# Two gate tiles of a state space decoder: half of their products computed inside the state space stage

## Chip, cores and metric

The kernel runs on one core of a Trainium2 chip. The metric is device time in microseconds (us) of one execution, the median of several runs. Lower is better. One execution was also recorded by the hardware profiler; all rows below are from it. TensorE is called PE, VectorE DVE, ScalarE ACT, GpSimd POOL, and SyncE, which issues most transfers, SP.

## The reference

A two-layer decoder trunk on one sequence of 1024 tokens with 1024 features: a diagonal state space layer with a gate, an MLP, a stick-breaking attention layer, a second MLP, with layer norms between. The change is in the first layer's mixer, cut here to what matters:

```python
def s5_mixer(x, w_in, ..., w_glu, b_glu, w_out):
    u = (x @ w_in).reshape(bsz, seq, S5_GROUPS, S5_GROUP)     # 64 groups of 16 channels
    ...
    _, _, s_re, s_im = lax.associative_scan(combine, (a_re, a_im, bu_re, bu_im), axis=0)
    y = (jnp.einsum('lbgp,ghp->blgh', s_re, c_re) - jnp.einsum('lbgp,ghp->blgh', s_im, c_im))
    y = (y + d_skip * u).reshape(bsz, seq, D_MODEL)
    g = jax.nn.gelu(y)
    out = g * jax.nn.sigmoid(g @ w_glu + b_glu)
    return out @ w_out
```

`g @ w_glu` is a product of 1024 x 1024 by 1024 x 1024; its sum over the 1024 input features runs over 8 tiles of 128 features.

## The kernel before

All large products are done in a three-product form: each operand is split into a high and a low part (`split`: a cast on ACT, a subtraction on DVE), and high times high, high times low and low times high are added in PSUM. A weight arrives by a transfer on SP's queue into a raw buffer (three of them, pool `wr`), is split into a slot of a weight pool (`wa` or `wb`, four slots each, a slot for 128 x 512 with both parts), and the raw buffer is free again.

**The state space stage** runs in 16 steps, one for each `Half` n of four groups (the loop from -3 to 16 overlaps three steps). The program text of a step has these parts: `into` and `scan` of half n+1 (PE: `p` from `U` and `V`; DVE: `R`, a scan, and then `Rs` and `Rc`), `y_mm` of half n (PE: `py`, 12 products from `Dm`, `Rc` and `Rs`), `kern` of half n+1 (PE: `pk`; ACT: four copies to `Dm`), transposes of half n+2 (`pU`, `pv`, copied by ACT to `U`, `V` and `Vs`), then the gelu of half n (ACT square `gs`, DVE, ACT tanh, DVE `zt`). After every second half, `z_out(i)` transposes a finished tile i of 128 features on PE (`pz`), and ACT and DVE write its high and low part, `gT_h` and `gT_l`. The gate reads `gT`.

Between those parts `fill` issues other work for PE. In steps before `NE` = 6 it is the rest of the input projection (`bunits`). In steps 6 to 14 it is nothing. In the last two steps it is the beginning of the gate (`gunits`, from `glu_ahead`): for the output tiles f = 0 and 1 the products of the feature tiles k = 0 to 6, six matmuls of 128x512 for one k (three products, two halves of the tokens), in numbers given by `GS`:

```python
def glu_ahead():
    for f in range(2):
        glu_ps(f)
        for k in range(KD - 1):
            dense_fm(pg[f], wg[f], gT, [k])
            yield
GS = (6, 1, 1, 1, 0), (3, 2, 0, 0, 0)
```

The weights of f = 0 and 1 are in `wa` from step 6 on.

**The gate** follows: k = 7 of f = 0 and 1, then f = 2 to 7 with all eight k. `glu_out(f)` does a sigmoid on ACT from PSUM (`gt`), a product with g on DVE (POOL has added up g in `zg`), and a split into `gg`. Weights are loaded two tiles ahead; those of f = 2 and 3 go into `wb`. After it come the output projection (`sopy`) and the MLP (`m0...`, where `wa` and `wb` take turns as slots for the weights).

The order of instructions on each engine is set by a scheduler from the program order and from when it takes buffers and inputs to be ready, so that an added part can also change the order of its neighbours. PSUM has eight banks: in this stage two for each of the tags `p12`, `pv`, `py` and `u`; `pz` uses `u`.

Of the kernel before, what the change touches and what calls it, by code (L numbers as in the profile page):

```python
# [9 lines left out]
F32 = mybir.dt.float32  # L10
# [35 lines left out]
def trunk(ctx, tc, A, out):  # L46
# [51 lines left out]
    def half(h):  # L98
        return slice(h * HF, (h + 1) * HF)
# [1 line left out]
    def tok(t):  # L101
        return slice(t * P, (t + 1) * P)

    def dense_fm(ps, w, xa, ks=range(KD), hs=(0, 1)):
        for k in ks:
            wh, wl = w[k]
            for h in hs:
                pe.matmul(ps[h], wh, xa[0][:, k, half(h)], start=(k == 0), stop=False)  # L108
            for h in hs:
                pe.matmul(ps[h], wh, xa[1][:, k, half(h)], start=False, stop=False)  # L110
            for h in hs:
                pe.matmul(ps[h], wl, xa[0][:, k, half(h)], start=False, stop=(k == KD - 1))
# [27 lines left out]
    class Slots:  # L140
# [8 lines left out]
        def next(self):  # L149
            self.n += 1  # L150
            return self.pools[(self.n - 1) % len(self.pools)]

        def of(self, src, name):

            return load_w(self.next(), None, name, HF, src)[0]

    def rows2(w, j, cols):

# [124 lines left out]
    with ExitStack() as ph:  # L283
# [380 lines left out]
                u_out(1, j, ps)  # L664


        wg, pg = {}, {}

        def glu_w(f):
            wg[f] = by_k(wsl.load(A["w_glu"][f], f"glu{f}"))  # L670
# [1 line left out]
        def glu_ps(f):  # L672
            pl, tag = ((ps1, "p12"), (ps1, "pv"), (ps1, "py"), (psu, "u"))[f % 4]
            pg[f] = [pl.tile([P, HF], F32, tag=tag, name=f"pg{f}{h}") for h in range(2)]

        def glu_ahead():
            for f in range(2):
                glu_ps(f)
                for k in range(KD - 1):
                    dense_fm(pg[f], wg[f], gT, [k])  # L680
                    yield

        tabs, zts = {}, {}
        NH = 2 * KD
        NE = 6
        GS = (6, 1, 1, 1, 0), (3, 2, 0, 0, 0)
        FS = (2,1,1,1,1)
        H = [Half(n) for n in range(NH)]
        for _ in stage_b([0]):
# [3 lines left out]
        for n in range(-3, NH + 1):  # L693
            cur = H[n] if 0 <= n < NH else None
            nx = H[n + 1] if 0 <= n + 1 < NH else None
            nx2 = H[n + 2] if 0 <= n + 2 < NH else None
            nx3 = H[n + 3] if n + 3 < NH else None

            def fill(i):
                if n < NE:  # L700
                    for _ in range(FS[i]):
                        next(bunits, None)
                elif n >= NH - 1:
                    for _ in range(GS[n - NH + 1][i]):
                        next(gunits, None)

            if n == NE:
                for _ in bunits:
                    pass
                rs_.close()  # L710
                gT = act_tiles(actp, "act", "gT")
                raws.append(mkpool(ctx, "wr", 3, side="right"))
                wa = mkpool(ctx, "wa", 4, side="right")
                wsl = Slots([wa] * 2)
                for f in range(2):
                    glu_w(f)
                gunits = glu_ahead()
            if nx3:
                load_bc(n + 3)
            if nx:  # L720
                nx.decay()
                nx.into()
                nx.scan()
            fill(0)
            if cur:
                cur.y_mm()
            fill(1)
            if nx:
                nx.kern()
            fill(2)  # L730
            if nx2:
                nx2.u_trans()
                nx2.v_coef()
            fill(3)
            if nx2:
                nx2.v_trans()
                nx2.w_coef()
            if cur:
                cur.gelu1()
            fill(4)  # L740
            if nx3 and nx3.hh == 0:
                tabs[nx3.i] = outer_tables(nx3.i)
            if n >= NE:
                if zwait:
                    z_out(zwait.pop(0))
            if cur:
                cur.gelu2()
            if cur and cur.hh == 1:
                zwait.append(cur.i)

    wb = mkpool(wbs, "wb", 4, side="right")
    wsl.pools += [wb] * 2


# [267 lines left out]
    class Down:  # L1022
# [21 lines left out]
        def tile(self, pl, nm_, tag):  # L1044
            return pl.tile([P, HF], F32, tag=tag, name=f"{self.nm}{nm_}")
# [274 lines left out]
    with ExitStack() as ph:  # L1320
        with ExitStack() as ph1:
            bp = mkpool(ph1, "ggp", 4)
            gg = act_tiles(bp, "gg", "gg")
            yst = ExitStack()
            yp = mkpool(yst, "yp", 8)
            y_tiles = [yp.tile([P, D], F32, tag="y", name=f"y0_{t}") for t in range(8)]
            with ExitStack() as ph2:
                zp = mkpool(ph2, "gz", 2)

                def glu_out(f, ps):  # L1330
                    for h in range(2):
                        z = zp.tile([P, HF], F32, tag="z", name=f"zg{f}{h}")
                        pool.tensor_add(z, gT[0][:, f, half(h)], gT[1][:, f, half(h)])
                        gt = zp.tile([P, HF], F32, tag="gt", name=f"gt{f}{h}")
                        act.activation(gt, ps[h], AF.Sigmoid, bias=bglu[:, f:f + 1])
                        dve.tensor_mul(gt, gt, z)

                        src = gt.rearrange("p (j c) -> p j c", j=4)
                        hv, lv = [v[:, f].rearrange("p (c j) -> p j c", j=8)[:, 4 * h:4 * h + 4] for v in gg]
                        split(hv, lv, src)  # L1340

                wo = []

                def ahead(i):
                    if i < KD:
                        glu_w(i)
                    else:
                        wo.append(wsl.load(rows2(A["w_out"], i - KD, half(0)), f"so0{i - KD}"))

                for f in range(KD):  # L1350
                    ahead(f + 2)
                    if f < 2:
                        dense_fm(pg[f], wg[f], gT, [KD - 1])
                    else:
                        glu_ps(f)
                        dense_fm(pg[f], wg[f], gT)
                    if f == KD - 1:
                        ahead(KD + 2)
                    glu_out(f, pg[f])
                ahead(KD + 3)  # L1360
            glu.close()

            def y_load(t):
                dma.dma_start(y_tiles[t], A["x"][tok(t)])

            xo = XOps(actp, "x1")
            w1 = []
            with ExitStack() as ph2:
                rest = proj_ln(ph2, flat(wo), lambda j: wsl.load(rows2(A["w_out"], j, half(1)), f"so1{j}"),
                               gg, xo, x_d[0], y_load, A["lnmg"][0], A["lnmb"][0], "so", y_tiles, w1_ahead(0, w1))  # L1370
            vpr = VProject()
            down = Down(0, "d0", x_d[0], wb, False, vpr)
            mlp_up(0, xo, y_tiles, w1, "m0", yst, bp, "gg", wb, "right", rest, down)
        with ExitStack() as ph1:
            x2T = down.run(ph1)
# [280 lines left out]
```

## Time and profile before

| | |
|---|---|
| runs, median of 3 | 2390.17 us (2385.36 to 2396.45) |
| profiled execution | 2393.1 us, span from first to last instruction 2391.4 us |
| PE busy | 2276.9 us, 95% of the span |
| DVE busy | 1838.9 us, 77% |
| ACT busy | 1234.1 us, 52% |
| POOL busy | 415.7 us, 17% |
| mean granted TensorE clock | 0.983 |

The shares are means over the whole span. The state space stage, the gate and the MLPs have different limits, so the stages have to be read apart. A busy time of PE sums records that overlap, because matmuls are pipelined; the pace of matmuls is read from their starts.

### The profile page before, as it was taken

The numbers are of one execution on the slowest core, as the hardware profiler recorded it, in microseconds if no ns is written. First come the engines' busy times: TensorE is split into PE (matmuls) and PEld (weight loads), VectorE is DVE, ScalarE is ACT, GpSimd is POOL, SyncE is SP. The second block draws the span as 40 slices with busy tenths as digits, with TensorE's granted clock in tenths as the row PEclk, the third lists the DMA queues.
The fourth block names the chain that finished last, engine by engine and source line by source line (L and its number), as shares of the span: only waits on it lengthen the run. The fifth ranks groups of instructions, "written<-read, shape, count | busy, mean of one in ns | idle before, by whom it ended". The sixth has DMA issues, their size and how long they took to land.

```text
span 2391.4 us, 32754 instructions
## 1 busy us (share of the span) xinstructions
PE 2276.9 (95%) x11072; PEld 1864.7 (78%) x11072; DVE 1838.9 (77%) x2887; ACT 1234.1 (52%) x2365; POOL 415.7 (17%) x709
## 2 busy tenths in 40 slices
PE   8997999999999999999999999988989999999996
PEld 7776878777888788888878878766867888788885
DVE  8899564886665888788179999896887666687888
ACT  6566441475555444444156777673366555544443
POOL 4000220021111000001144444341002111100002
PEclk9998999999999999999999999999999999999998
DMA  4222231385444944536655554465457434665432
GB/s 148 65 78 54 68 105 66 137 276 182 145 148 161 316 129 146 150 97 185 128 130 120 127 124 112 117 144 190 141 182 277 154 146 145 231 201 167 134 114 106
DMA packets 195448, 349.38 MB, mean 146 GB/s; under 512 B 23248, under 2 KB 66256, under 8 KB 195280
## 3 DMA queue, kind: packets, MB, share of 16 engines
q1 hardware_dynamic: 136400, 246.61, 33.0%
q0 software_dynamic: 58880, 100.69, 15.2%
q8 instruction: 87, 1.43, 0.3%
q14 instruction: 81, 0.66, 0.1%
HBM read 212.96 MB, written 100.66 MB: 131 GB/s over the span
## 4 chain that ended last, share of the span: by engine, by line
PE 59%; DVE 14%; issue 12%; DMA 5%; ACT 4%; POOL 4%; SPq 0%; POOLq 0%; DVEq 0%; ACTq 0%
PE d0M L1109 4%; PE d0M L1111 4%; PE d0M L1110 4%; PE d1M L1109 4%; PE d1M L1111 4%; PE d1M L1110 4%; DVE qq L1470 2%; PE m0A L847 2%; PE m0A L846 2%; PE m0A L845 2%; DVE be L1471 2%; POOL h_d L939 2%; PE po L1497 1%; PE pg L108 1%; PE pg L110 1%
## 5 line engine op out<-in xcount | busy, mean ns | idle before, releaser
L1470 DVE TENSOR_TENSOR_SCAN qq<-qq 128x128 f32<-128x128 f32 (+7 forms) x128 | 173.8, 1360 | 11.4 <-POOL qq L1464 11.2
L1109 PE MATMUL d1M<-w_d12M,w_d1HM 128*128 128x512 f32 x448 | 175.0, 392 | 2.6 <-DVE d1y L1118 2.6
L1109 PE MATMUL d0M<-w_d02M,w_d0HM 128*128 128x512 f32 x448 | 174.6, 390 | 1.4 <-ACT w_d02M L122 1.0
L1111 PE MATMUL d1M<-w_d12M,w_d1HM 128*128 128x512 f32 x448 | 175.2, 391 | 0.0
L1110 PE MATMUL d1M<-w_d12M,w_d1HM 128*128 128x512 f32 x448 | 174.7, 390 | 0.0
L1110 PE MATMUL d0M<-w_d02M,w_d0HM 128*128 128x512 f32 x448 | 174.5, 390 | 0.0
L1111 PE MATMUL d0M<-w_d02M,w_d0HM 128*128 128x512 f32 x448 | 174.3, 389 | 0.0
L122 ACT CAST w_d0HM<-d0hM 128x512 fp32r<-128x512 f32 x110 | 68.3, 621 | 169.0 <-PE d0M L1111 140.0
L122 ACT CAST w_d1HM<-d1hM 128x512 fp32r<-128x512 f32 x110 | 68.3, 621 | 168.2 <-PE d1M L1111 136.1
L122 ACT CAST wTh<-pt 128x512 fp32r<-128x512 f32 (+1 forms) x192 | 88.0, 485 | 82.7 <-PE pt L1483 82.1
L1483 PE MATMUL pt<-ident,be 128*128 128x128 f32 x576 | 91.0, 282 | 35.4 <-DVE wTl L123 26.5
L1483 PEld LDWEIGHTS pt<-ident,be 128*128 128x128 f32 x576 | 70.0, 144 | 61.8 <-issue 15.5
L123 DVE TENSOR_TENSOR w_d1HM<-d1hM,w_d1HM 128x512 fp32r<-128x512 f32 x110 | 75.8, 690 | 52.5 <-ACT w_d1HM L122 52.2
L194 POOL TENSOR_TENSOR rsd<-ved,nhalf 128x1 f32<-128x1 f32 x16 | 11.3, 710 | 602.8 <-DVE ved L192 593.6
L123 DVE TENSOR_TENSOR w_d0HM<-d0hM,w_d0HM 128x512 fp32r<-128x512 f32 x110 | 75.8, 689 | 51.6 <-ACT w_d0HM L122 51.5
L123 DVE TENSOR_TENSOR wTl<-pt,wTh 128x512 fp32r<-128x512 f32 (+1 forms) x192 | 99.4, 543 | 11.2 <-ACT wTh L122 11.2
L1471 DVE TENSOR_TENSOR be<-be,qq 128x127 f32<-128x127 f32 (+7 forms) x128 | 99.4, 777 | 6.6
L1461 ACT ACTIVATE qq<-pz 128x512 f32<-128x512 f32 (+1 forms) x192 | 96.7, 504 | 10.8 <-DVE be L1471 5.9
L1109 PEld LDWEIGHTS d1M<-w_d12M,w_d1HM 128*128 128x128 f32 x448 | 84.1, 188 | 23.1 <-ACT d1y L196 2.0
L1109 PEld LDWEIGHTS d0M<-w_d02M,w_d0HM 128*128 128x128 f32 x448 | 84.1, 188 | 21.2 <-DVE d0y L1118 2.4
L1111 PEld LDWEIGHTS d1M<-w_d12M,w_d1HM 128*128 128x128 f32 x448 | 84.1, 188 | 18.3
L1110 PEld LDWEIGHTS d1M<-w_d12M,w_d1HM 128*128 128x128 f32 x448 | 84.1, 188 | 17.7
(482 smaller groups left out, 7077.2 us busy)
## 6 DMA issues: line engine op xcount, KB each, us to landing
d0hM<-h_d SPq DMA_DIRECT2D x110, 256.0 KB, 2.7
d1hM<-h_d SPq DMA_DIRECT2D x110, 256.0 KB, 2.7
x1ring<-in_w SPq DMA_DIRECT2D x70, 256.0 KB, 3.2
x3ring<-in_w SPq DMA_DIRECT2D x70, 256.0 KB, 3.1
h_d<-m0hs POOLq DMA_DIRECT2D x64, 256.0 KB, 2.8
h_d<-m1hs POOLq DMA_DIRECT2D x64, 256.0 KB, 2.7
d0r<-in_w SPq DMA_DIRECT2D x58, 256.0 KB, 3.6
d1r<-in_w SPq DMA_DIRECT2D x58, 256.0 KB, 3.2
```

The source lines that it names most:

```text
L122: act.copy(hi, src)
L123: dve.tensor_sub(lo, src, hi)
L845: pe.matmul(ps_, wh, xh[:, k], start=first and k == 0, stop=False, skip_group_check=True)
L846: pe.matmul(ps_, wh, xl[:, k], start=False, stop=False, skip_group_check=True)
L847: pe.matmul(ps_, wl, xh[:, k], start=False, stop=k == 3, skip_group_check=True)
L1109: pe.matmul(ps_, hh[:, tok(t)], wh, start=first, stop=False, skip_group_check=True)
L1110: pe.matmul(ps_, hh[:, tok(t)], wl, start=False, stop=False, skip_group_check=True)
L1111: pe.matmul(ps_, hl[:, tok(t)], wh, start=False, stop=last, skip_group_check=True)
L1461: act.activation(qq[:, s0:s1], pz, AF.Sigmoid, scale=-0.125)
L1470: dve.tensor_tensor_scan(out=rev, data0=rev, data1=rev, initial=1.0, op0=ALU.mult, op1=ALU.bypass)
L1471: dve.tensor_mul(be[:, 0:ns - 1], be[:, 0:ns - 1], qq[:, 1:ns])
L1483: pe.transpose(pt[:, b_], self.be[:, tok(s0 + b_)], ident)
```

## The change

Half of the products of f = 0 and 1, those of k = 0 to 3 (`KH` = 4), move out of `glu_ahead` into a new generator, `glu_first`. It goes through f and the two halves of the tokens h, and for each of the four pairs adds 4 x 3 = 12 matmuls of 128x512 in one bank of the tag `u` (names `pgf`); ACT copies the sum to a slot of 128 x 512 in f32 (`pgs`). It gives way after every two k, so that one call issues six matmuls. `fill` calls it twice a step (parts 0 and 2) in steps 10 to 14. `glu_ahead` begins at k = 4, and `GS` is shorter. `glu_out` adds `pgs` to the PSUM sum on DVE ahead of the sigmoid.

The slots for `pgs` are two of the four slots of `wb`: these are opened early as a pool of their own (`wba`), the other two (`wbb`) at the old place, and `Both` hands out slots of the two pools in turn.

```diff
-    def dense_fm(ps, w, xa, ks=range(KD), hs=(0, 1)):
+    def dense_fm(ps, w, xa, ks=range(KD), hs=(0, 1), begin=0):
...
-                pe.matmul(ps[h], wh, xa[0][:, k, half(h)], start=(k == 0), stop=False)
+                pe.matmul(ps[h], wh, xa[0][:, k, half(h)], start=(k == begin), stop=False)
...
+    class Both:
...
+        def tile(self, *a, **k):
+            self.n += 1
+            return self.pools[(self.n - 1) % 2].tile(*a, **k)
...
+        KH = KD // 2
...
+        def glu_first():
+            for f in range(2):
+                s_ = wba.tile([P, 2, HF], F32, tag="w", name=f"pgs{f}")
+                for h in range(2):
+                    ps = psu.tile([P, HF], F32, tag="u", name=f"pgf{f}{h}")
+                    for k in range(KH):
+                        wh, wl = wg[f][k]
+                        for i, (w, x) in enumerate(((wh, gT[0]), (wh, gT[1]), (wl, gT[0]))):
+                            pe.matmul(ps, w, x[:, k, half(h)], start=k + i == 0, stop=k == KH - 1 and i == 2)
+                        if k % 2:
+                            yield
+                    pgs[f, h] = s_[:, h]
+                    act.copy(pgs[f, h], ps)
...
-                for k in range(KD - 1):
-                    dense_fm(pg[f], wg[f], gT, [k])
+                for k in range(KH, KD - 1):
+                    dense_fm(pg[f], wg[f], gT, [k], begin=KH)
                     yield
...
-        GS = (6, 1, 1, 1, 0), (3, 2, 0, 0, 0)
+        GS = (2, 1, 1, 0, 0), (2, 0, 0, 0, 0)
...
+                elif n > NH // 2 + 1 and i in (0, 2):
+                    next(gfirst, None)
...
+                wba = mkpool(wbs, "wba", 2, side="right")
+                gfirst = glu_first()
...
-    wb = mkpool(wbs, "wb", 4, side="right")
+    wb = Both([mkpool(wbs, "wbb", 2, side="right"), wba])
...
+                        if (f, h) in pgs:
+                            dve.tensor_add(ps[h], ps[h], pgs[f, h])
```

Three places show what moves. The first is PE in step 12 to 13, at the transposes after `pk` and ahead of the products from `Rc` of half 13. Before:

```order
L581 MATMUL pk_2411<-WW_2337,VT_121 32x112
L594 MATMUL pU_2428<-ident,u_323 128x128 x4
L653 MATMUL pz_2456<-ident,zt_2253 128x128 x4
L653 MATMUL pz_2463<-ident,zt_2253 128x128 x4
L629 MATMUL py_2499<-Dm_117,U_2321 128x8x16
L630 MATMUL py_2499<-WW_2337,Rc_2390 128x8x16
```

And now (line numbers are 10 higher here, `py` from `Rc` is the last row):

```order
L591 MATMUL pk_2451<-WW_2368,VT_121 32x112
L696 MATMUL pgf_2429<-gT_h_1658,w_glu_1678 128x512
L696 MATMUL pgf_2429<-gT_l_1660,w_glu_1678 128x512
...
L604 MATMUL pU_2474<-ident,u_323 128x128 x4
L663 MATMUL pz_2502<-ident,zt_2270 128x128 x4
L663 MATMUL pz_2509<-ident,zt_2270 128x128 x4
L639 MATMUL py_2553<-Dm_117,U_2352 128x8x16
L696 MATMUL pgf_2546<-gT_h_1658,w_glu_1678 128x512
L696 MATMUL pgf_2546<-gT_l_1660,w_glu_1678 128x512
...
L640 MATMUL py_2553<-WW_2368,Rc_2421 128x8x16
```

Six of the moved matmuls stand ahead of the transposes and eleven directly ahead of the first product from `Rc`. In the steps before, the other units stand in and after `pk` (12, steps 10 to 11), behind `p` (6) and around `pU` (12, steps 11 to 12); one single matmul follows `pk` of the step after. In both steps that start with such a wait for `Rc`, `pv` and `p` now also stand two to three `py` products later in the row than before.

The second place is ACT at the seam to the gate, from the last `gT_h` on. Before:

```order
L655 ACTIVATE gT_h_1659<-pz_2750 128x512
L122 CAST w_glu_2784<-r_glu_2785 128x512
L122 CAST w_glu_2789<-r_glu_2790 128x512
L122 CAST w_glu_2814<-r_glu_2815 128x512
L1335 ACT_TABLE_LOAD
L1335 ACTIVATE gt_2802<-pg_2637,bglu 128x512
L1335 ACTIVATE gt_2809<-pg_2638,bglu 128x512
```

And now:

```order
L665 ACTIVATE gT_h_1659<-pz_2763 128x512
L122 CAST w_glu_2797<-r_glu_2798 128x512
L122 CAST w_glu_2829<-r_glu_2830 128x512
L1367 ACT_TABLE_LOAD
L1367 ACTIVATE gt_2816<-pg_2698,bglu 128x512
L122 CAST w_glu_2802<-r_glu_2803 128x512
L1367 ACTIVATE gt_2824<-pg_2699,bglu 128x512
```

The cast of the second half of the weights of f = 2 (`w_glu_2789`, now `w_glu_2802`) moves behind the first sigmoid.

The third place is DVE there, from the last `gT_l` on. Now:

```order
L666 SCALAR_TENSOR_TENSOR gT_l_1661<-pz_2763,gT_h_1659 128x512
L123 TENSOR_TENSOR w_glu_2797<-r_glu_2798,w_glu_2797 128x512
L1363 TENSOR_TENSOR pg_2698<-pg_2698,pgs_2182 128x512
L1363 TENSOR_TENSOR pg_2699<-pg_2699,pgs_2182 128x512
L123 TENSOR_TENSOR w_glu_2829<-r_glu_2830,w_glu_2829 128x512
L1363 TENSOR_TENSOR pg_2733<-pg_2733,pgs_2428 128x512
L1363 TENSOR_TENSOR pg_2734<-pg_2734,pgs_2428 128x512
L1368 TENSOR_TENSOR gt_2816<-gt_2816,zg_2814 128x512
L123 TENSOR_TENSOR w_glu_2802<-r_glu_2803,w_glu_2802 128x512
```

The four additions are new; the subtraction for that second half of the weights, which was the second row after `gT_l`, is now behind them and behind the first product of the gate.

## Rows read from the trace of the kernel before

**Rows 1.** The page's first part, busy us, share and count by engine.

```profile
PE 2276.9 (95%) x11072; PEld 1864.7 (78%) x11072; DVE 1838.9 (77%) x2887; ACT 1234.1 (52%) x2365; POOL 415.7 (17%) x709
```

**Rows 2.** Windows: length; busy us of PE, PEld, DVE, ACT, POOL; granted clock; transfers.

```profile
110.00:140.00 30.00, 29.42 (x214) 23.86 (x213) 28.07 (x44) 20.63 (x50) 0.64 (x6) 1.00 0.26 62
...
199.00:259.00 60.00, 46.09 (x347) 42.72 (x348) 55.12 (x85) 35.61 (x83) 1.06 (x10) 0.83 0.19 44
259.00:283.00 24.00, 23.75 (x123) 19.61 (x120) 4.43 (x8) 5.29 (x12) 2.55 (x2) 1.00 0.12 39
283.00:354.00 71.00, 70.46 (x301) 56.25 (x302) 49.30 (x50) 37.60 (x51) 26.26 (x14) 1.00 0.35 116
```

**Rows 3.** Waits of DVE from 199 to 259: us in total, times, longest.

```profile
DVE R L609 <- PE p L603: 1.9, 3, 0.9
DVE v L610 <- PE p L605: 1.4, 3, 0.8
DVE gT_l L656 <- ACT gT_h L655: 0.9, 1, 0.9
DVE zt L646 <- ACT gs L639: 0.4, 1, 0.4
```

**Rows 4.** Waits of PE from 199 to 259.

```profile
PE py L630 <- DVE Rc L624: 8.9, 2, 4.6
PE py L629 <- ACT Dm L589: 3.9, 4, 1.7
```

**Rows 5.** Waits of DVE from 84 to 170, the steps with filling.

```profile
DVE zt L646 <- ACT gs L639: 3.7, 4, 1.1
DVE R L609 <- PE p L603: 0.3, 1, 0.3
```

**Rows 6.** PE in order of time: start, us, operation, idle before it.

```profile
212.99 0.76 PE L630 MATMUL py<-WW,Rc 128*128 128x128 f32 x2 [4.55 <-DVE Rc L624]
...
215.36 2.07 PE L603 MATMUL p<-U,V 128*128 128x128 f32 x8
217.23 1.09 PE L605 MATMUL p<-U,Vs 128*128 128x128 f32 x8
```

**Rows 7.** PE in order of time, the last two steps of the stage.

```profile
259.31 0.71 PE L108 MATMUL pg<-gT_h,w_glu 128*128 128x512 f32 x2
...
271.87 0.63 PE L108 MATMUL pg<-gT_h,w_glu 128*128 128x512 f32 x2
...
281.20 0.63 PE L112 MATMUL pg<-gT_h,w_glu 128*128 128x512 f32 x2
281.67 1.04 PE L653 MATMUL pz<-ident,zt 128*128 128x128 f32 x8
```

**Rows 8.** Waits from 259 to 285, two of the longest.

```profile
ACT gT_h L655 <- PE pz L653: 9.7, 1, 9.7
...
ACT gs L635 <- PE py L632: 8.2, 1, 8.2
```

**Rows 9.** DVE in order of time, end of the stage.

```profile
254.54 0.69 DVE L609 TENSOR_TENSOR R<-p,C 128x512 f32<-128x512 f32 x1 [0.76 <-PE p L603]
...
259.42 0.68 DVE L624 TENSOR_TENSOR Rc<-R,C 128x508 f32<-128x508 f32 x1
...
262.09 1.28 DVE L656 SCALAR_TENSOR_TENSOR gT_l<-pz,gT_h 128x512 fp32r<-128x512 f32 x2
...
272.68 0.69 DVE L646 SCALAR_TENSOR_TENSOR zt<-gs,py 128x512 f32<-128x512 f32 x1 [0.70 <-ACT gs L639]
```

**Rows 10.** ACT in order of time.

```profile
259.10 1.70 ACT L589 COPY Dm<-pk 32x512 f32<-32x512 f32 x4
...
270.67 0.60 ACT L635 ACTIVATE gs<-py 128x512 f32<-128x512 f32 x1 [8.23 <-PE py L632]
...
...
286.25 1.27 ACT L1335 ACTIVATE gt<-pg,bglu 128x512 f32<-128x512 f32 x2
```

**Rows 11.** Waits of PE from 520 to 560, in the first MLP.

```profile
PE m0A L845 <- DVE m0hA L942: 2.4, 2, 1.8
```

More of the change, by code (lines that the diff above doesn't have):

```diff
@@ L155, in of, with __init__ @@
             return load_w(self.next(), None, name, HF, src)[0]
+    class Both:
+        def __init__(self, pools):
+            self.pools, self.n = pools, 0
+        def tile(self, *a, **k):
+            self.n += 1
+            return self.pools[(self.n - 1) % 2].tile(*a, **k)
     def rows2(w, j, cols):
@@ L664, in stage_b @@
                 u_out(1, j, ps)
-        wg, pg = {}, {}
+        wg, pg, pgs = {}, {}, {}
+        KH = KD // 2
         def glu_w(f):
```

## Prediction

> **What bounds the kernel now.** I read the page's first part, then windows by stage, then the waits of each stage, then PE, DVE and ACT in order of time around the seam between the state space stage and the gate. PE is busy 95% of the span [rows 1], which suggests that only fewer or faster matmuls can help. The windows say that this isn't so everywhere [rows 2]. From 259 us on PE is full: 23.75 of 24 us in the last two steps of the stage, 70.46 of 71 in the gate. From 199 to 259, steps 10 to 14, it is busy 46.09 of 60 at a granted clock of 0.83, and DVE 55.12 of 60. So in these steps DVE's chain sets the pace, and PE has 13.9 us without a record, besides the time that it loses at the lower clock.
>
> Where these 13.9 us lie is seen in PE's waits [rows 4]: 8.9 us in two waits of up to 4.6 for `Rc`, which DVE has to finish, and 3.9 us in four for `Dm`, which ACT copies. What they do to the clock is seen behind one of them [rows 6]: after 4.55 us of idle time eight products for `p` take 2.07 us and the next eight 1.09, so the first ran at 1.2 GHz and the second at 2.4. DVE then waits for these `p`: 1.9 us and 1.4 us in all [rows 3], beside 0.9 for `gT_h` and 0.4 for the tanh, 4.6 us together.
>
> At the seam the roles change. PE works through 84 gate matmuls without a gap while the last two links of the stage's chain stand behind them in its queue: ACT waits 8.2 us for `py` of the last half and 9.7 us for the last `pz` [rows 8]. The inputs of that `py` were there long before: `Rc` ends at 260.1 [rows 9], `Dm` at 260.8 [rows 10].
>
> **The change, term by term.**
>
> *The pace.* From 271.87 to 281.20 PE starts 40 matmuls of 128x512 (20 rows of two, 0.467 us apart), 9.33 / 40 = 0.233 us each [rows 7]. Their recorded 0.39 us overlap and aren't the price.
>
> *Removed at the seam.* Of 14 units of six matmuls (7 for each f), 8 go, 48 matmuls: 48 x 0.233 = 11.2 us. They count in full only if nothing else then ends last. I followed the chain anew. The first `pg` starts at 259.3; two units take 2.8 us, to 262.1, later than `Rc` (260.1) and `Dm` (260.8). `py` of the last half follows. Before, six units (8.4 us) brought PE to 267.7 and `gs` began at 270.67 [rows 10], 3.0 us for `py` and the way to ACT; now `gs` begins at 265.1. The last `zt` ended at 273.4 [rows 9], 2.7 us after that start, so now at 267.8. PE meanwhile has four more units, 5.6 us, to 270.3 or 270.5; so `pz` is again held by PE's queue and not by its input. The unit behind `py` needs tile 6 of `gT`, whose low part ends at 263.4 [rows 9], also in time. `pz` starts at about 270.4 instead of 281.67. PE has no gap, and the whole 11.2 us is gone from its row at this place.
>
> *Added in steps 10 to 14.* The same 48 matmuls, 11.2 us at 2.4 GHz, 22.4 at 1.2. I compare with the 13.9 us that are free. By the new order, 12 stand in and behind `pk` ahead of a wait for `Rc` (4.55 us before), 6 behind `p` and 12 around `pU`, and 17 around the other wait for `Rc` (4.4 us before), the last one behind the next `pk`. All have a gap behind or around them. What lies behind them on PE is `pU` and `pz` (wanted later by ACT) and in two steps `pv` and `p`, which the scheduler has moved two or three `py` products back.
>
> The trace before has a stretch with filling already: from 110 to 140 PE is busy 29.42 of 30 and the granted clock is 1.00 [rows 2]. There DVE waited only 0.3 us for `p` in 86 us, but 3.7 us for the tanh, which `py` delays [rows 5]; on 60 us this is 4.0 x 60 / 86 = 2.8 us. Against the 4.6 us of steps 10 to 14 the stage would get shorter by 1.8. The bounds of this term: at best all 4.6 us of DVE's waits go; at worst no gap takes a unit and the stage grows by 11.2 us at full clock or 22.4 at half. I take the filled stretch, as it is the nearest: -1.8.
>
> On this the Trainium skill has a rule, in "TensorE: Matmul & The Clock Gate", section "Part 1: The HAM clock gate (the "warmup" mystery)": the array's default is the throttled clock, and activity releases it. The trace agrees, with 0.83 and half-speed products behind gaps, and 1.00 where PE is filled [rows 2, 6]. By it alone the added units would keep PE at 2.4 GHz in all of steps 10 to 14, and the sum would be that of the first rival below, 2375.0.
>
> *ACT's four copies.* None is in the trace, but ACT's `gs`, also 128x512 from PSUM to SBUF in f32, takes 0.60 us [rows 10]. Three have slack on ACT (busy 35.61 of 60 [rows 2]). The one of step 13 stands between `Dm` and `gT_h`, for which DVE waited 0.9 us already [rows 3]: +0.6. A copy also frees the bank that the next `pz` needs, since `u` has two; this falls into the wait for `Rc`, and costs nothing while that lasts.
>
> *DVE's four additions in the gate.* About 0.69 us each, as another operation with one operand in PSUM [rows 9]. DVE is busy 49.3 of 71 us in the gate [rows 2] and PE doesn't wait for the sigmoid of f = 0 before f = 4, whose banks it frees: nothing. But they stand in front of the weights. PE reaches f = 2 when k = 7 of f = 0 and 1 is done, and its second half of the weights 24 matmuls, 5.6 us, later. DVE has to do two additions, a subtraction, two additions, one gate product and then the subtraction in question, seven operations at about 0.6 us from start to start, 4.2 us; ACT's sigmoid (1.27 for two [rows 10]) and a cast lie beside it. That leaves 1.4 us. I take 0; if the cover is gone, PE waits 1 or 2 us there once.
>
> *Transfers.* SP's queue holds the same transfers. The raw buffer of that second half is freed some 4 us later than before, so that the transfers of f = 4 go out later, but they have f = 2 and 3, 22 us, to land in. Nothing.
>
> *The pool of two and two.* In the first MLP `Both` hands out slots in strict turn, and the scheduler swaps a few products of `m0A` and `m0C`. PE had 2.4 us of waits there [rows 11]; these may go or double. I take 0 with 2.4 either way.
>
> The sum: -11.2 - 1.8 + 0.6 = -12.4 us. The profiled execution, 2393.1 (span 2391.4), would become 2380.7; the median of the runs shown, 2.9 lower, 2390.2 - 12.4 = **2377.8**.
>
> **The rivals.**
>
> *The clock stays up in all of steps 10 to 14.* Then no `p` comes late and the chain of `py`, `Dm`, `pv`, `p` at the end of the stage, where DVE itself waits, runs at twice the speed: all 4.6 us of DVE's waits [rows 3] go, 11.2 + 4.6 - 0.6 = 15.2, 2375.0. (The page of the Trainium skill named above, "TensorE: Matmul & The Clock Gate", section "Part 1", speaks for it.) For it in the rows: 1.00 in the filled stretch. Against it: there were 18 added matmuls a step there, here about ten, and an idle rest of 1.5 to 2 us ahead of each `Rc` remains by my count. 0.2.
>
> *The units get in the way.* `pv` and `p` are later in PE's row, and if the clock has fallen when `Rc` comes, the moved products ahead of `p` cost two or three times 0.43 us, and the unit behind `p` delays `py`, `gs` and `Dm` by up to 2.8 us in a step. Two odd steps with about 1.5 us and two even ones with 1 us give 5 us back: 11.2 - 5 = 6.2, 2384. For it: DVE is at 92%, so any lateness counts. 0.21.
>
> *The kept sums hold back the gate's weights.* If the slots come free late, f = 2 and 3 wait for their second halves, some 2 us each, 2382. 0.05.
>
> *Slower.* The units run at 1.2 GHz and none is absorbed: 22.4 us added ahead of what DVE waits for, 11.2 saved, 2390.2 + 11.2 = 2401. It decides from the point at which steps 10 to 14 grow by more than 11.2 us. Against it: the two waits for `Rc` alone are 8.9 us, and they end when DVE is done, whatever PE does in them. 0.04.
>
> *The change doesn't do what it says*: the order shows the 48 matmuls moved, so only the first term's size can be off.
>
> **How the numbers follow.** My forecast, 2375.5 to 2381, has 0.5. The rivals have 0.2, 0.21, 0.05 and 0.04. Faster by over 0.5% means below 2378.2, and 0.5% is about what a measurement of this kernel can tell from no change; the forecast lies at that bound. Somewhat more than half of its 0.5 and all of the first rival are below it: 0.48. The slower rival gives 0.04, the rest is 0.48. The range reaches from the best case with the MLP's 2.4 us and some spread of runs, 2371, to the second rival's and a little over, 2385.5.
>
> **What would show it.** Right: `pz` of the last tile starts within 2 us of PE's last unit and some 11 to 13 us earlier; the granted clock from 199 to 259 is over 0.9; DVE's waits there for `p` under 2 us; no wait of PE for `w_glu` at f = 2; the gate's 71 us and all later stages as long as before. Wrong: DVE's last `Rc` ends later than 260.1, by as much as the gain lacks; or a new PE wait at f = 2; or an MLP that is some us longer.

## The result and the profile after

The changed kernel takes 2373.29 us, the median of 6 runs (2371.49 to 2377.32), beside 2388.23 us (2385.36 to 2396.45) of the kernel before on the same chip. The ratio is 0.9934, 95% interval 0.9923 to 0.9945, a gain of 14.9 us or 0.63%. The forecast of 2377.8 was 4.5 us too high: 1.9 of them lie in the kernel before, whose median was 2390.17 when the forecast was made, and 2.5 in the gain, 14.9 instead of 12.4. The time lies in the range of 2371 to 2385.5, but below the narrower 2375.5 to 2381 that had a chance of 0.5, and nearest to the rival in which the clock stays up (2375.0).

The profiled execution took 2371.73 us, its span 2369.9. The first part of its page, busy us, share and count by engine, answers to [rows 1]: the same 11072 matmuls, four more instructions on DVE and on ACT.

```profile
PE 2268.2 (96%) x11072; PEld 1857.0 (78%) x11072; DVE 1842.2 (78%) x2891; ACT 1235.6 (52%) x2369; POOL 415.3 (18%) x709
```

Windows of the changed kernel, columns as in [rows 2]. Its step 10 begins at 197.2 us (198.9 before), so its steps 10 to 14 are the second row, the last two steps the third, the rest of the gate the fourth.

```profile
110.00:140.00 30.00, 29.43 (x216) 24.02 (x215) 27.98 (x44) 20.80 (x51) 0.42 (x4) 1.00 0.27 65
197.00:254.00 57.00, 50.75 (x399) 44.67 (x400) 54.63 (x85) 38.25 (x89) 1.05 (x10) 1.00 0.20 47
254.00:268.00 14.00, 13.75 (x76) 11.42 (x75) 6.36 (x11) 6.47 (x14) 2.55 (x2) 1.00 0.21 67
268.00:337.00 69.00, 68.54 (x294) 54.73 (x292) 50.43 (x51) 35.61 (x48) 30.02 (x14) 1.00 0.37 119
```

The granted clock in steps 10 to 14 is 1.00, where it was 0.83. PE has some 50 records more there, the moved work, and yet the steps are shorter. The waits of DVE in them, as in [rows 3] (us in total, times, longest), are 2.2 us instead of 4.6; those for `p` have gone from 3.3 to 1.0.

```profile
DVE gT_l L666 <- ACT gT_h L665: 1.2, 1, 1.2
DVE R L619 <- PE p L613: 0.8, 1, 0.8
DVE v L620 <- PE p L615: 0.2, 1, 0.2
```

The waits of PE, as in [rows 4]: 8.9 us for `Rc` have become 2.6.

```profile
PE py L640 <- DVE Rc L634: 2.6, 3, 1.8
PE py L639 <- ACT Dm L599: 2.3, 2, 1.4
```

PE in order of time at the longest of them, as in [rows 6]. It still stands idle for 1.79 us, but the eight products for `p` behind it take 1.10 us, where they took 2.07: in this execution the products behind the gap ran at the upper level of 2.4 GHz. (The other of the two long waits, 4.35 us before, is down to 0.18.)

```profile
211.30 0.46 PE L640 MATMUL py<-WW,Rc 128*128 128x128 f32 x2 [1.79 <-DVE Rc L634]
211.60 0.39 PE L642 MATMUL py<-W,Rs 128*128 128x128 f32 x2
...
213.37 1.10 PE L613 MATMUL p<-U,V 128*128 128x128 f32 x8
214.31 1.06 PE L615 MATMUL p<-U,Vs 128*128 128x128 f32 x8
```

The seam, PE in order of time, as in [rows 7]:

```profile
253.81 0.71 PE L108 MATMUL pg<-gT_h,w_glu 128*128 128x512 f32 x2
...
256.69 0.38 PE L639 MATMUL py<-Dm,U 128*128 128x128 f32 x2
...
264.50 0.63 PE L112 MATMUL pg<-gT_h,w_glu 128*128 128x512 f32 x2
264.97 1.04 PE L663 MATMUL pz<-ident,zt 128*128 128x128 f32 x8
```

From the first `pg` to the last `pz` PE needs 264.97 - 253.81 = 11.16 us; it was 281.67 - 259.31 = 22.36. The difference is 11.20 us, 48 x 0.233. The waits around it answer to [rows 8]: both links of the chain still stand behind PE's queue, for 4.1 and 2.6 us instead of 9.7 and 8.2.

```profile
ACT gT_h L665 <- PE pz L663: 4.1, 1, 4.1
...
ACT gs L645 <- PE py L642: 2.6, 1, 2.6
...
PE pg L108 <- ACT gT_h L665: 0.2, 1, 0.2
```

DVE's chain shows the gain of the steps as well. Its last `Rc` ended 61.2 us after the first `py` of step 10 (260.1 - 198.9) and now ends 58.1 us after it (255.3 - 197.2), 3.0 us sooner:

```profile
254.66 0.68 DVE L634 TENSOR_TENSOR Rc<-R,C 128x508 f32<-128x508 f32 x1
```

Where did the time go? From the first `py` of step 10 to the first `pg` it was 60.4 us and is 56.6 (-3.8). The seam gives -11.2. The gate, from the last `pz` to the first `sopy`, takes 72.1 us in both. The output projection and the first MLP, from `sopy` to `d0M`, go from 424.7 to 422.0 (-2.7), all later stages together give -2.1, and steps before 10, which the change does not touch, -1.7. The sum, -21.5 us, is that of the two profiled executions; their own times are 2393.1 and 2371.7, each near one end of its runs. The medians are 14.9 us apart, so several us of these small terms belong to the executions and not to the change. The experiments have to say which.

### The profile page after: what moved, and what is told of

Same layout as the page of the kernel before. It is cut to its first block, busy times and chain, and to the rows that moved or that the text cites. A ratio compares the mean times of both kernels' runs of the same rounds, so it can differ in the third digit from the quotient of the medians.

```text
span 2369.9 us, 32760 instructions
## 1 busy us (share of the span) xinstructions
PE 2268.2 (96%) x11072; PEld 1857.0 (78%) x11072; DVE 1842.2 (78%) x2891; ACT 1235.6 (52%) x2369; POOL 415.3 (18%) x709
## 3 DMA queue, kind: packets, MB, share of 16 engines
q8 instruction: 87, 1.43, 0.3%
## 4 chain that ended last, share of the span: by engine, by line
PE 59%; DVE 16%; issue 11%; DMA 6%; ACT 4%; POOL 4%; SPq 1%; POOLq 0%; DVEq 0%; ACTq 0%
PE d0M L1139 4%; PE d0M L1141 4%; PE d0M L1140 4%; PE d1M L1139 4%; PE d1M L1141 4%; PE d1M L1140 4%; DVE qq L1502 2%; PE m0A L877 2%; PE m0A L876 2%; PE m0A L875 2%; DVE be L1503 2%; PE po L1529 2%; POOL h_d L969 1%; PE pt L1515 1%; PE pg L108 1%
## 5 line engine op out<-in xcount | busy, mean ns | idle before, releaser
L1502 DVE TENSOR_TENSOR_SCAN qq<-qq 128x128 f32<-128x128 f32 (+7 forms) x128 | 174.0, 1362 | 11.8 <-POOL qq L1496 11.5
L123 DVE TENSOR_TENSOR wTl<-pt,wTh 128x512 fp32r<-128x512 f32 (+1 forms) x192 | 99.6, 544 | 11.3 <-ACT wTh L122 11.2
L1139 PEld LDWEIGHTS d1M<-w_d12M,w_d1HM 128*128 128x128 f32 x448 | 84.1, 188 | 22.8 <-ACT d1y L206 2.0
L1139 PEld LDWEIGHTS d0M<-w_d02M,w_d0HM 128*128 128x128 f32 x448 | 84.1, 188 | 21.4 <-DVE d0y L1148 2.5
L1141 PEld LDWEIGHTS d1M<-w_d12M,w_d1HM 128*128 128x128 f32 x448 | 84.1, 188 | 18.3
L1494 ACT ACTIVATE be<-pz 128x512 f32<-128x512 f32 (+1 forms) x192 | 98.1, 512 | 0.0
```

What stands on the lines that cost most here:

```text
L123: dve.tensor_sub(lo, src, hi)
L1139: pe.matmul(ps_, hh[:, tok(t)], wh, start=first, stop=False, skip_group_check=True)
L1141: pe.matmul(ps_, hl[:, tok(t)], wh, start=False, stop=last, skip_group_check=True)
L1494: act.activation(be[:, s0:s1], pz, AF.Sigmoid, scale=0.125)
L1502: dve.tensor_tensor_scan(out=rev, data0=rev, data1=rev, initial=1.0, op0=ALU.mult, op1=ALU.bypass)
```

## The experiments

The theory after the result: two gains that add up. The seam loses its 48 matmuls of queue, and steps 10 to 14 take the same matmuls in without cost and keep the clock up on top. Rivals: the seam alone did it and the steps are as before; the order of the instructions around the units, not their work, made the steps shorter; or the pool of two and two moved the MLP.

Each ratio below is to runs of the kernel before on the same chip, with its 95% interval.

### The seam alone, and the filling alone

`seam_only` is the kernel before without the products of k = 0 to 3 of f = 0 and 1, with the changed kernel's `GS`; nothing is added in steps 10 to 14.

```diff
-                for k in range(KD - 1):
-                    dense_fm(pg[f], wg[f], gT, [k])
+                for k in range(4, KD - 1):
+                    dense_fm(pg[f], wg[f], gT, [k], begin=4)
                     yield
...
-        GS = (6, 1, 1, 1, 0), (3, 2, 0, 0, 0)
+        GS = (2, 1, 1, 0, 0), (2, 0, 0, 0, 0)
```

> Leaves out the products of k = 0 to 3 of f = 0 and 1 altogether: the seam is as short as in the changed kernel, and nothing is added to steps 10 to 14. Theory (two gains that add up: 11.2 us at the seam, about 4 us because filled steps keep the clock up): the granted clock in steps 10 to 14 stays near 0.83, the steps take about 60 us as before, the seam is 11.2 us shorter, time 11 us below the kernel before, about 2377. Rival A (the seam gives everything, the stage nothing): 15 us below, about 2373, like the changed kernel. Rival B (the added work costs the stage, hidden by something else): below the changed kernel, under 2371.

Measured: 2378.36 us, ratio 0.9950 (0.9935 to 0.9964) to 2389.0, a gain of 10.6 us. Its windows, steps 10 to 14 and the seam:

```profile
197.70:257.60 59.90, 45.94 (x350) 42.56 (x351) 55.50 (x86) 35.92 (x84) 1.04 (x10) 0.83 0.19 48
257.60:268.90 11.30, 11.30 (x65) 9.61 (x64) 4.06 (x7) 4.31 (x9) 2.55 (x2) 1.00 0.20 59
```

The steps are those of before, 59.9 us at a clock of 0.83. The seam is 11.2 us from first `pg` to `pz`. So the seam is worth what the prediction's first term says, and stands by itself.

`fill_only` is the counterpart: the changed kernel with all of the seam's matmuls in place again, and the kept sums multiplied by 0.

```diff
-                for k in range(KH, KD - 1):
-                    dense_fm(pg[f], wg[f], gT, [k], begin=KH)
+                for k in range(KD - 1):
+                    dense_fm(pg[f], wg[f], gT, [k])
...
-        GS = (2, 1, 1, 0, 0), (2, 0, 0, 0, 0)
+        GS = (6, 1, 1, 1, 0), (3, 2, 0, 0, 0)
...
-                            dve.tensor_add(ps[h], ps[h], pgs[f, h])
+                            dve.scalar_tensor_tensor(ps[h], pgs[f, h], 0.0, ps[h], op0=ALU.mult, op1=ALU.add)
```

> The changed kernel with the seam of before: the units in steps 10 to 14, the copies, the slots and the four additions stay (with the kept sums multiplied by 0), and all k of f = 0 and 1 are multiplied at the seam again. Theory: granted clock 1.00 in steps 10 to 14, which take some 57 us in place of 60, the seam as long as before; time about 4 us below the kernel before, 2384. Rival A (the stage gives nothing): 2388. Rival B (the units cost): 2390 or more.

Measured: 2383.56 us, ratio 0.9976 (0.9964 to 0.9988), 5.4 us faster although it does 48 matmuls more than the kernel before.

```profile
196.60:253.30 56.70, 50.62 (x399) 44.52 (x399) 54.32 (x85) 37.98 (x88) 1.06 (x10) 1.00 0.20 47
253.30:275.80 22.50, 22.50 (x112) 18.60 (x111) 4.75 (x8) 4.25 (x9) 2.55 (x2) 1.00 0.13 42
```

The steps are the changed kernel's (56.7 us, clock 1.00), the seam is the old one. 10.6 + 5.4 = 16.0 beside 14.9 for the whole change: two gains that add up within the intervals. The intervals are wide, though: 2.9 to 8.6 us for the filling alone. On top of the shorter seam it isn't clear of the noise, with ratios of 0.9934 and, measured again below, 0.9946 for the whole change beside 0.9950 for `seam_only`.

### The same instructions with little work

`fill_tiny` is `fill_only` with each of the added matmuls on 16 columns instead of 512, and the copies and additions too. Instructions and weight loads stay, the work goes. The order stays in part: around the two later waits for `Rc`, at halves 13 and 14, PE has the order of the changed kernel, but at halves 11 and 12 the scheduler has put `pv` and `p` back among the `py` products about where the kernel before has them.

```diff
-                            pe.matmul(ps, w, x[:, k, half(h)], start=k + i == 0, stop=k == KH - 1 and i == 2)
+                            pe.matmul(ps[:, :16], w, x[:, k, h * HF:h * HF + 16], start=k + i == 0, stop=k == KH - 1 and i == 2)
...
```

> fill_only with each of the 48 added matmuls on 16 columns in place of 512, and copies and additions as small: the same instructions in almost the same order on each engine, but little work for PE. Theory (the clock is what shortens the stage): clock back near 0.83, steps 10 to 14 about 60 us, time as before, 2388. Rival C (it is the new order of instructions on PE, ACT and DVE that shortens the stage): steps 10 to 14 about 57 us, time 2384 as fill_only.

Measured: 2387.92 us, ratio 0.9996 (0.9985 to 1.0007), no gain. Its window of steps 10 to 14, DVE's waits there, and PE and DVE in order of time at half 13:

```profile
197.00:257.50 60.50, 50.58 (x399) 46.95 (x399) 54.47 (x85) 36.39 (x89) 1.06 (x10) 0.89 0.19 44
```

```profile
DVE R L619 <- PE p L613: 5.2, 2, 2.9
```

```profile
236.12 0.76 PE L640 MATMUL py<-WW,Rc 128*128 128x128 f32 x2 [1.50 <-DVE Rc L634]
240.09 1.91 PE L613 MATMUL p<-U,V 128*128 128x128 f32 x8
242.04 0.69 DVE L619 TENSOR_TENSOR R<-p,C 128x512 f32<-128x512 f32 x1 [2.94 <-PE p L613]
```

DVE waits 5.2 us for `p`, in two places, 2.94 us at 242.0 and 2.23 at 253.6. Both lie where the order is that of the changed kernel, which waits there not at all and 0.76 us; from `pk` of half 13 to `pk` of half 15 `fill_tiny` takes 27.6 us and the changed kernel 23.8. So in these two steps the order without the work gives nothing: `p` comes late because its products and those ahead of it run at half speed. In the two steps in which the order was not kept, both kernels take as long as each other (24.9 and 25.0 us), so what the order gives there was not tested.

### The pool of two and two

```diff
-    wb = mkpool(wbs, "wb", 4, side="right")
+    wba = mkpool(wbs, "wba", 2, side="right")
+    wb = Both([mkpool(wbs, "wbb", 2, side="right"), wba])
```

> The kernel before with the four slots of wb in two pools of two that take turns, and nothing else changed. Between the profiled executions of before and of the change, the first MLP is 2.3 us shorter. Theory D (strict turns of the slots and the order of products that comes of them): MLP shorter by 2 us here too, time about 2386. Rival (spread between executions): MLP as before, 2388.

Measured: 2387.12 us, ratio 0.9990 (0.9977 to 1.0003), which can't be told from the kernel before. From `sopy` to `d0M` it took 422.5 us, beside 424.7 before and 422.0 after. But `seam_only`, with the old pool, took 423.4, so at most 1 or 2 us are the pool's. Its window of steps 10 to 14 holds a warning:

```profile
195.00:252.40 57.40, 43.15 (x350) 39.56 (x351) 55.50 (x86) 36.28 (x85) 1.06 (x10) 0.91 0.21 53
```

Nothing is filled in here, and yet these steps took 57.5 us at a clock of 0.91, 2.9 less than in the kernel before. The edit was not neutral there: the scheduler moved `pv` of half 15 behind three more `py` products, nearly where the changed kernel has it. Three kernels with the order of the kernel before in these steps (the kernel before, `seam_only` and, below, `shift_before`) took 60.4, 59.9 and 60.3 us, each at 0.83. So part of what the filled steps gain may come from the order of `pv` and `p`; the median of `pools_only`, 1.9 us below the kernel before and not clear of it, leaves room for up to 5.5 us.

The filled steps are not always as short as in the changed kernel either. `shift_after`, a run below with the changed kernel's instructions in the same order (only its tiles lie 32 bytes later), took 59.7 us for them in its profiled execution, at a clock of 0.94. There too PE stood idle for 1.80 us ahead of `Rc`, but the products that followed ran at half speed (0.62 us for a row of two where the changed kernel has 0.39), and later DVE waited 2.28 us for `p`:

```profile
197.70:257.40 59.70, 53.62 (x398) 47.60 (x399) 54.58 (x85) 37.83 (x88) 1.05 (x10) 0.94 0.19 44
```

```profile
211.78 0.48 PE L641 MATMUL py<-WW,Rc 128*128 128x128 f32 x2 [1.80 <-DVE Rc L635]
212.08 0.62 PE L643 MATMUL py<-W,Rs 128*128 128x128 f32 x2
...
253.53 0.69 DVE L620 TENSOR_TENSOR R<-p,C 128x512 f32<-128x512 f32 x1 [2.28 <-PE p L614]
```

Over all kept traces the granted clock of these steps is 0.83 to 0.91 without the added work or with little of it, and 0.94 to 1.00 with it; the times, 57.5 to 60.4 us and 56.6 to 59.7 with the units of the change alone, overlap. How much the filling saves is therefore better read from medians (5.4 us, 2.9 to 8.6) than from one pair of traces.

### More filling

`change_again` is the changed kernel once more, as a companion of the next three.

> The changed kernel unaltered, as a base for the three others. About 2373.

Measured: 2376.20 us, ratio 0.9946 (0.9930 to 0.9962), a gain of 11.5 us. The interval overlaps that of the first measurement (14.9 us), so 12 to 15 us is what is known of the size.

`five_tiles` moves five feature tiles instead of four.

```diff
-        KH = KD // 2
+        KH = 5
-        GS = (2, 1, 1, 0, 0), (2, 0, 0, 0, 0)
+        GS = (1, 1, 1, 0, 0), (1, 0, 0, 0, 0)
```

> Five feature tiles in place of four move into steps 10 to 14 (60 matmuls in place of 48; two units fewer at the seam for k = 4). Theory (the seam is PE's queue until the last py and zt are its limit; steps 10 to 14 have 6 us of PE free): the seam 12 x 0.233 = 2.8 us shorter, steps 10 to 14 as long, time 2370.5. Rival (the longer hold on one of the two banks of tag u delays pz, and p stands behind units in PE's row): steps 10 to 14 longer by 2 to 3 us, 2373.

Measured: 2371.13 us, ratio 0.9931 (0.9917 to 0.9946), not told apart from the change. PE in order of time at its seam:

```profile
256.50 0.70 PE L108 MATMUL pg<-gT_h,w_glu 128*128 128x512 f32 x2
...
265.02 1.03 PE L663 MATMUL pz<-ident,zt 128*128 128x128 f32 x8
```

The seam is 8.5 us, 2.6 shorter, as 12 matmuls less should make it. But it begins 2.7 us later, 0.7 because step 10 did and 2.0 because the steps are longer, so `pz` comes at the same time as in the changed kernel (264.97). The 2.0 us have two possible causes that this run doesn't separate. From `pk` of half 11 to `pk` of half 12 the kernel takes 17.2 us instead of 14.8, and there four products for `pz` now stand among those for `p`; but also the products that followed a gap of 1.43 us ran at half speed, at a granted clock of 0.97 over the steps:

```profile
212.00 0.49 PE L640 MATMUL py<-WW,Rc 128*128 128x128 f32 x2 [1.43 <-DVE Rc L634]
212.30 0.62 PE L642 MATMUL py<-W,Rs 128*128 128x128 f32 x2
```

`fill_double` adds to the changed kernel 60 more matmuls in steps 10 to 14, ten units at the parts 1 and 3, whose sums are copied by one column and added times 0.

```diff
...
+                elif n > NH // 2 + 1 and i in (1, 3):
+                    next(gdummy, None)
...
```

> The changed kernel with 60 more matmuls of 128x512 in steps 10 to 14, six at two further parts of each step (their sums enter the result times 0): 14.0 us of PE work. This is the rival in which units get in the way, brought about. In the changed kernel PE has 6 us without a record in these steps. Theory: PE becomes full, and the steps grow by at least 14.0 - 6 = 8 us, time 2381 or a few us more. Rival (DVE still sets the pace): 2373 to 2375.

Measured: 2381.46 us, ratio 0.9973 (0.9963 to 0.9984), 5 to 8 us slower than the change. Its window of the steps:

```profile
199.00:261.00 62.00, 61.09 (x442) 52.47 (x442) 55.15 (x85) 39.76 (x100) 1.07 (x10) 1.00 0.20 50
```

PE is full now (61.1 of 62 us) and the first `pg` comes at 261.2, 7.4 us later than with the change alone. 60 matmuls are 14 us at 0.233; about half of them found room.

### A gain from elsewhere

`fill_earlier` adds to the changed kernel six units of six matmuls in steps 7 to 9, where the clock was 0.88 in the changed kernel (from 170 to 199 us).

```diff
+        dcol = cst.tile([P, 6], F32, name="dcol")
...
+                act.copy(dcol[:, j:j + 1], ps[:, 0:1])
...
+                elif n > NE and i in (0, 2):
+                    next(gdummy, None)
...
```

> The changed kernel with 36 more matmuls of 128x512 in steps 7 to 9, six at a time at the same parts of the step (their sums enter the result times 0). Theory (the clock shortens unfilled steps): granted clock in steps 7 to 9 from 0.88 to 1.00, DVE's waits for p there gone, 1 to 2 us below the changed kernel, 2372, in spite of 8.4 us more work for PE. Rival (in steps 10 to 14 it was something else): the added work costs or does nothing, 2373 or more.

Measured: 2363.49 us, ratio 0.9893 (0.9877 to 0.9910), 10 to 13 us faster than the change and far more than expected. The clock in steps 7 to 9 did rise to 1.00, but they took as long as before (37.4 us, 37.2 in the changed kernel), and the first `pg` came at 254.75, no earlier than in the changed kernel (253.81). A higher clock did not shorten these steps. So the gain lay behind the stage. It showed in windows in which PE is full: the first fence has three of the changed kernel, in the gate, the output projection and the first MLP, the second that of `fill_earlier` in the first MLP:

```profile
280.00:320.00 40.00, 40.00 (x173) 32.15 (x172) 30.96 (x30) 20.69 (x28) 19.09 (x10) 1.00 0.37 116
345.00:375.00 30.00, 30.00 (x131) 24.14 (x130) 8.25 (x12) 2.49 (x4) 0.00 (x0) 1.00 0.11 36
...
600.00:700.00 100.00, 100.00 (x430) 80.36 (x429) 61.83 (x93) 56.60 (x93) 19.43 (x36) 1.00 0.43 150
```

```profile
600.00:700.00 100.00, 100.00 (x438) 82.05 (x437) 62.89 (x95) 57.50 (x95) 20.81 (x39) 1.00 0.45 156
```

In the first MLP 438 matmuls start in the time of 430, at the same granted clock of 1.00 and the same order of instructions: one every 0.229 us instead of 0.233. The added code had one effect there: the small tile `dcol` of 6 columns in the pool of constants, 32 bytes with its padding, lets every tile allocated behind it on that side of SBUF begin 32 bytes later. By the programs' allocation, the kernel before and the changed kernel place the activations at multiples of 64 bytes and these weights 32 past one. Three kernels tell the address from the filling.

`shift_after` is the changed kernel with only this shift; `shift_before` has the same edit in the kernel before:

```diff
-    nhalf = cst.tile([P, 1], F32, name="nhalf")
+    nhalf = cst.tile([P, 9], F32, name="nhalf")
     dve.memset(nhalf, -0.5)
+    nhalf = nhalf[:, :1]
```

`fill_even` is `fill_earlier` with a shift of 64 bytes:

```diff
-        dcol = cst.tile([P, 6], F32, name="dcol")
+        dcol = cst.tile([P, 12], F32, name="dcol")
```

> The changed kernel with its tile of constants nhalf 9 columns wide instead of 1, of which one is used: every tile allocated after it on that side of SBUF begins 32 bytes later, and nothing else differs. It is for the unexpected gain of the version with 36 added multiplications in steps 7 to 9, whose consumed column tile shifted the same tiles by 32 bytes too. Theory, the addresses made that gain: the multiplications of the first MLP half come every 0.229 us instead of every 0.2333 us, on some 1,350 of them -6 us, with those of pjk and pjq -9 at most; the run takes 2366 to 2370 us, ratio to the kernel before 0.990 to 0.9925. Rival, the added work in steps 7 to 9 made it: the pace stays at 0.2333 us and the run takes what the changed kernel took, 2373 to 2376 us, ratio 0.9934 to 0.9946.

> The version with 36 added multiplications in steps 7 to 9 (their sums multiplied by 0), with its tile of consumed columns 12 wide instead of 6, so that the later tiles begin 64 bytes later than in the changed kernel instead of 32. Theory of the addresses: the gain is gone, the pace of the first MLP half is 0.2333 us again, 2373 to 2377 us, ratio 0.9934 to 0.995. Rival of the added work: 2363 us as before, ratio 0.989, at a pace of 0.229.

> The kernel before with nhalf 9 columns wide, so that the same tiles begin 32 bytes later. Theory of the addresses: the pace of the first MLP half falls from 0.2333 to 0.229 us and the run is 6 to 9 us faster than the kernel before, ratio 0.996 to 0.9975, without any part of the change. Rival: ratio 1.000.

Measured, all beside 2389.18 us: `shift_after` 2367.76, ratio 0.9902 (0.9884 to 0.9920); `fill_even` 2374.05, 0.9933 (0.9918 to 0.9949); `shift_before` 2381.28, 0.9961 (0.9946 to 0.9976). The shift made the gain, and the filling in steps 7 to 9 none that can be told from zero. Windows of `shift_after` in the gate, the output projection and the MLP:

```profile
280.00:320.00 40.00, 40.00 (x177) 32.81 (x176) 30.36 (x31) 22.01 (x30) 20.75 (x11) 1.00 0.41 132
345.00:375.00 30.00, 30.00 (x130) 24.20 (x129) 8.25 (x12) 2.48 (x4) 0.00 (x0) 1.00 0.12 37
...
600.00:700.00 100.00, 100.00 (x438) 82.05 (x437) 62.89 (x94) 57.39 (x94) 20.28 (x38) 1.00 0.44 153
```

Beside the changed kernel's three rows above, the gate (177 for 173) and the MLP (438 for 430), whose 512-column operand is an activation that has moved, are faster by 2%. The output projection (130 for 131), whose 512-column operand is a weight on the other side that has not moved, is as before. In `fill_even` the window from 600 to 700 holds 430 again, in `shift_before` 438. The change itself moves none of these tiles: 600 to 700 holds 430 matmuls in the kernel before too. `shift_after` beats both kernels, 21.4 us below the kernel before.

## Why the prediction was right, step by step

**The bound.** Right: steps 10 to 14 at DVE's pace with late `p`, the seam in PE's queue. `seam_only` and `fill_only` take the two apart.

**Removed at the seam, -11.2.** Right, and to the size: 11.20 us in the trace, 10.6 in the medians of `seam_only`. `gs` and the last `pz` are held by PE's queue as the prediction followed them; the last `pz` follows PE's last unit without a gap, 16.7 us earlier than before.

**Added in steps 10 to 14, -1.8.** That the filling shortens the steps was right, the term was mis-sized: with the copies, -1.8 + 0.6 = -1.2 was forecast and `fill_only` measured -5.4 in medians (2.9 to 8.6), and the profiled executions show -3.8. The step that failed is "I take the filled stretch, as it is the nearest". It carried 2.8 us of waits for the tanh over from steps that take in 18 matmuls each; with about ten they are not there (no such wait among those shown from 197 to 254). Twelve in a step brought some back, one of the two behind products at half speed: in `five_tiles` DVE waits 1.9 us for the tanh.

The argument against the first rival failed too, in the changed kernel's own trace: an idle rest of 1.79 us remained ahead of one `Rc` (0.18 ahead of the other of the two), and the granted clock was 1.00 all the same. So that rival's clock is what this execution shows. Its sum is right in part by luck: it let all 4.6 us of DVE's waits go, and 2.4 went (4.6 to 2.2). What the Trainium skill says in "TensorE: Matmul & The Clock Gate", section "Part 1: The HAM clock gate (the "warmup" mystery)", that activity releases the throttle, spoke for that rival. The runs agree in direction: 1.00 with the full added work, 0.89 with the same instructions and little work. That the clock then stays up throughout they do not bear out: 0.94 in `shift_after`, where the products behind a gap of 1.80 us ran at half speed.

**ACT's four copies, +0.6.** About +0.3: DVE's wait for `gT_h` is 1.2 us, 0.9 before. The late banks show as 0.5 us of PE's wait for `pz`.

**DVE's additions, and the weights behind them, 0.** Right: PE has no wait for `w_glu` from 253 to 285, and the gate takes 72.1 us in both.

**Transfers, 0.** Right by the same gate.

**The pool of two and two, 0 with 2.4 either way.** Held: the `pools_only` interval contains no change. The two waits for `m0hA` have gone and one of 2.0 us for a weight of `m0C` has come. Whether the 1 to 2 us that the first MLP is shorter are the pool's stays open.

**The other rivals.** Units in the way, kept sums that hold back weights, and units at half clock did not show in the changed kernel. The first of them does come with more filling: in `fill_double` PE is full and the time goes up. In `five_tiles` it may be part of the 2.0 us by which the steps grow.

The two parts measured alone, -10.6 and -5.4, have the copies in them and add up to -16.0, beside -14.9 and -11.5 in the two measurements of the change. That filling pays is shown by `fill_only`, and that it is the work and not the instructions' presence or order by `fill_tiny` for two of the four halves around which the order changed. Not shown is how much of the rest the new order of `pv` and `p` gives, nor in how many executions the clock stays up.

## What to carry to other kernels

Work that stands in a full queue at the end of a stage can be moved into an earlier stretch where the engine waits, and it may pay twice: once in the queue, and once where the granted clock rises with the added work (0.83 to 1.00 here) and the chain's own small products come back in time. Take the second gain as a chance and not as certain, as a kernel with the same order of instructions showed 0.94. Read the room from the waits; of ten added units too many, half came back as time. An edit elsewhere can change the order of instructions in a stage, as in `pools_only`, so compare the orders before a difference there is put down to chance. When a variant is faster for no visible reason, count the matmuls in a stretch where PE is full: a pace that has changed points to where the tiles lie, not to the schedule.

## What the runs showed of the hardware

The pace of matmuls with 512 columns depends on where in SBUF their tiles begin. A shift of the activations by 32 bytes brought it from 0.233 to 0.229 us at the same granted clock (430 to 438 matmuls in 100 us), and the run 6 to 8 us down in the changed kernel and 8 in the kernel before; a shift by 64 bytes did not. Which operand's address counts, and with respect to what, stays open: the output projection kept its pace, and the second half of the MLP (`d0M`) runs at 0.227 us in all kernels here.

Behind idle gaps of nearly the same length, with the same instructions in the same order, TensorE's products ran at either level of its clock: at the upper level behind 1.79 us in the changed kernel, at half speed behind 1.80 us in `shift_after`. In the kernel before, behind 4.55 us, they ran at half speed. Steps 10 to 14 took 56.6 and 59.7 us in these two executions, at granted clocks of 1.00 and 0.94. The tiles of `shift_after` lie 32 bytes later; whether that plays a part was not tested.
